# Convolutions of the latent tokens begun ahead of the layer's other convolutions, and a skip row by products

## The chip, the cores and the metric

The kernel is one program on 1 core of a Trainium2 chip. The metric is the device time of one execution in microseconds (us). The core's engines run side by side, each with its own in-order queue: TensorE (PE, matrix products; its weight loads are shown apart as PEld), VectorE (DVE), ScalarE (ACT), GpSimd (POOL) and SyncE (SP), which issues most DMAs.

## The reference

A backbone of two layers over 2,048 latent tokens and 256 context tokens, 1,024 wide. Layer 0 is attention beside a Hyena branch (two gated long convolutions), layer 1 two kinds of local attention. What the change touches lies in layer 0:

```python
def hyena_branch(u, conv_w, conv_b, w1, b1, w2, b2, freq, w3, d_skip):
    n = u.shape[1]
    filt = hyena_filters(n, w1, b1, w2, b2, freq, w3)
    uc = centred_depthwise_conv(u, conv_w, conv_b)
    parts = jnp.split(uc, HYENA_ORDER + 1, axis=-1)
    z = parts[0]
    for o in range(HYENA_ORDER):
        z = parts[o + 1] * bidir_long_conv(z, filt[:, o, 0], filt[:, o, 1], d_skip[o])
    return z

def bidir_long_conv(z, h_fwd, h_bwd, d_skip):
    n = z.shape[1]
    taps = jnp.concatenate([h_fwd, jnp.zeros_like(h_fwd[:1]), h_bwd[:0:-1]], axis=0)
    taps = taps * lax.rsqrt(jnp.sum(taps * taps, axis=0, keepdims=True) + EPS)
    zf = jnp.fft.rfft(z.astype(jnp.float32), n=2 * n, axis=1)
    tf = jnp.fft.rfft(taps, n=2 * n, axis=0)
    y = jnp.fft.irfft(zf * tf[None], n=2 * n, axis=1)[:, :n]
    return (y + z.astype(jnp.float32) * d_skip.astype(jnp.float32)).astype(z.dtype)
```

The modulation of each layer is `silu(cond) @ w_ada + b_ada`, split into shift, scale and gate; the projection is `modulated_norm(x) @ w_in`.

## The kernel before

Layer 0's projection runs in three groups of tokens (GRP: 768 each, as blocks of 512 and 256). For a group, `ln0` normalizes and transposes the tokens into `hT`; `kvq` makes keys, values and queries (products `psA`); `us` makes the 1,536 columns of the Hyena branch, 512 at a time, into `u0` in DRAM; `gates` makes two gates of 512 columns into `g0` (both products `psB`, L222; DVE or ACT empty the banks, L339 to L342). A product of two fp32 numbers is three products of fp32r halves, so each piece of `w_in` is loaded (`wraw`), rounded on ACT (`whi`, L243) and its rest made on POOL (`wlo`, L244). Three raw pieces of 256 KB are in flight.

`filters` (L450 on), during group 0 and 1, makes the long filters. Their first tap gets the skip weight: `d_skip` divided by the filter's norm. The norm is one number per channel; its channels lie across partitions, four to a partition (`ssv`, 128x4), while the tap's row (`first`) has 512 channels on one partition. L524 writes the four columns to DRAM (`rD`), L526 reads them back as a row, L528 loads the skip weights, L529 and L530 multiply and add. That is done four times: two filters, for the context (`ctxt` 1) and for the latent tokens (0).

Between groups 1 and 2 the program has the context's attention and Hyena branch and then, in pool `ad1`, the modulation's sums: `ada_sum` (L94, L95) multiplies the conditioning with `w_ada`'s last 1,024 columns of layer 0 and all 3,072 of layer 1. The three PSUM tiles `pa` that hold the sums are the whole of tag "x" (3 banks) in pool `xp`. The weights come through two slots of 128 x 3,072 (`adaw`), 1.5 MB each.

`gate_convs` convolves the last 512 columns of `u0` (pieces of 512 tokens, `gu` and `gy`) into `zG`. `latent_conv` convolves the other two parts: a unit is one block of 128 channels and a half of the tokens, loaded with a margin (`u`, 512.5 KB). ACT scales the middle tap (L721), DVE adds the two others (L723), all three writing the view `prm`, in which token n*64+s stands at s*32+n, so that neighbouring tokens are 128 bytes apart. There are 16 units: two parts, two halves of the channels (`ch`), two blocks in each and two halves of the tokens. PE transposes the result (`ptz`, L733); part 0 is stacked (`zst`, L380, L381), put through the first transform (`hpA`, L669, L670, in tag "x") and stored in `XA`; part 1 is stored in `zD`. The attention of layer 0 and the rest of the Hyena branch follow behind the first maxima (`pm`, L888), at about 1,180 us.

The kernel is written for a build that sets the order of instructions on each engine itself: a scheduler goes by the place in the program as priority, by what each instruction needs, and by its own durations. So work from several places of the program stands interleaved on an engine. Slots of a tile are given out in turn (`bufs`): a load into one waits, on the queue that issues it, until the last use of what was there.

## Time and profile before

| | us |
|---|---|
| median of three timed runs | 3899.59 |
| lowest, highest | 3898.86, 3904.81 |
| the profiled execution | 3905.59 |
| its span, first to last instruction | 3903.8 |
| PE busy | 3627.0 (93%) |
| DVE busy | 2305.7 (59%) |
| ACT busy | 1802.8 (46%) |
| POOL busy | 1733.5 (44%) |

Busy time is the union of an engine's instructions; issuing a DMA or waiting does not count. A releaser is what ended an engine's idle time. PEclk is the clock granted to PE, as a share of 2.4 GHz; a stretch at 0.5 runs at 1.2 GHz.

### The profile page before, as it was taken

Reading aid. Unit: us, or ns where it says so; the run is one execution under the profiler, and the core shown is the slowest. Engines: PE = TensorE matmul, PEld = TensorE weight load, DVE = VectorE, ACT = ScalarE, POOL = GpSimd, SP = SyncE. Lnnn points to the kernel's source line nnn. Section 1 sums busy time; section 2 is a strip of 40 time slices with the busy share of each in tenths; the row PEclk is TensorE's granted clock in tenths of the full one; section 3 lists DMA queues with packets and bytes.
Section 4 is the critical chain, followed back from the end, with each engine's and each line's share of the span. In section 5 each row is a group of like instructions: output and inputs, shape, how many; then the busy total and the mean of one; then the engine's idle time right before and its main releaser. Section 6 shows DMA issues by size and latency. Waiting matters only on the chain.

```text
span 3903.8 us, 57140 instructions
## 1 busy us (share of the span) xinstructions
PE 3627.0 (93%) x20080; PEld 2615.3 (67%) x20080; DVE 2305.7 (59%) x4370; ACT 1802.8 (46%) x3482; POOL 1733.5 (44%) x1433
## 2 busy tenths in 40 slices
PE   6799989997788999999998989999998999999999
PEld 2588767756574554455545657887876878888887
DVE  6754762626877775677664338286158267677622
ACT  4554652413535665566453334344233266666610
POOL 1444552213245786767797555353244222132310
PEclk9899999999898999999999999999999999999999
DMA  6444344465567555343343454555465375365355
GB/s 197 93 135 132 134 119 119 135 215 191 164 182 221 172 163 185 119 144 117 108 161 112 135 159 139 168 168 152 139 191 160 118 180 139 91 161 133 112 175 168
DMA packets 536337, 586.23 MB, mean 150 GB/s; under 512 B 71318, under 2 KB 362448, under 8 KB 531954
## 3 DMA queue, kind: packets, MB, share of 16 engines
q1 hardware_dynamic: 519778, 551.12, 48.5%
q10 hardware_dynamic: 13856, 25.18, 1.7%
q0 software_dynamic: 2416, 6.29, 0.6%
q8 instruction: 158, 2.59, 0.3%
q14 instruction: 129, 1.06, 0.1%
HBM read 389.63 MB, written 192.76 MB: 149 GB/s over the span
## 4 chain that ended last, share of the span: by engine, by line
PE 59%; DVE 8%; DMA 5%; issue 5%; ACT 3%; POOL 2%; SPq 0%; ACTq 0%; POOLq 0%; DVEq 0%
PE psB L222 8%; PE pso L222 7%; PE psA L222 6%; PE po L994 6%; PE npt L1569 4%; PE no L1581 4%; PE pS L975 4%; PE pm L888 3%; PE pS L976 3%; PE ns L1550 2%; PE ns L1556 2%; PE hpX L802 1%; PE hpC L795 1%; PE hpH L807 1%; DMA wraw<-in_w_in_dram 1%
## 5 line engine op out<-in xcount | busy, mean ns | idle before, releaser
L244 POOL TENSOR_TENSOR wlo<-wraw,whi 128x512 fp32r<-128x512 f32 x368 | 500.9, 1376 | 832.8 <-ACT whi L243 657.5
L989 POOL TENSOR_TENSOR pacc<-pacc,Pt 128x512 f32<-128x512 f32 x512 | 646.0, 1284 | 193.1 <-ACT Pt L977 191.4
L222 PE MATMUL psB<-hT,whi 128*128 128x512 f32 (+1 forms) x2560 | 667.1, 350 | 29.5 <-DVE u L714 8.9
L222 PE MATMUL psA<-whi,hT 128*128 128x512 f32 (+1 forms) x1952 | 571.3, 373 | 34.1 <-DVE u L717 11.3
L222 PEld LDWEIGHTS psB<-hT,whi 128*128 128x128 f32 x2560 | 451.9, 193 | 107.6 <-issue 13.1
L889 DVE TENSOR_REDUCE mx<-pm 128x1 f32<-128x512 f32 (+1 forms) x640 | 389.6, 631 | 185.5 <-PE pm L888 181.3
L977 ACT ACTIVATE Pt<-pS 128x512 f32<-128x512 f32 x576 | 332.9, 597 | 351.8 <-PE pS L976 326.1
L222 PE MATMUL psB<-hT,wlo 128*128 128x512 f32 (+1 forms) x1280 | 442.2, 351 | 8.0 <-POOL wlo L244 7.8
L222 PEld LDWEIGHTS psA<-whi,hT 128*128 128x128 f32 x1952 | 356.8, 193 | 103.5 <-DVE u L717 11.5
L243 ACT CAST whi<-wraw 128x512 fp32r<-128x512 f32 x368 | 222.0, 618 | 312.3 <-DMA wraw<-in_w_in_dram 141.4
L222 PE MATMUL psA<-wlo,hT 128*128 128x512 f32 (+1 forms) x976 | 356.6, 370 | 0.8 <-POOL wlo L244 0.5
L222 PE MATMUL pso<-whi,oy 128*128 128x512 f32 x1088 | 344.2, 395 | 9.1 <-DMA oy<-yT 8.2
L975 PE MATMUL pS<-Q,K 128*128 128x512 f32 x576 | 331.2, 575 | 10.2 <-ACT Pt L977 9.5
L994 PE MATMUL po<-Pt,V 128*64 128x512 f32 x1152 | 287.2, 621 | 0.0
L222 PEld LDWEIGHTS psB<-hT,wlo 128*128 128x128 f32 x1280 | 245.9, 193 | 46.8 <-POOL wlo L244 12.1
L1569 PE MATMUL npt<-ident,np 128*128 128x128 f32 x1488 | 258.2, 283 | 3.3 <-DVE ggt L1153 1.9
L975 PEld LDWEIGHTS pS<-Q,K 128*128 128x128 f32 x576 | 110.1, 191 | 205.2 <-issue 99.8
L222 PEld LDWEIGHTS pso<-whi,oy 128*128 128x128 f32 x1088 | 205.9, 190 | 60.4 <-issue 7.6
L976 PE MATMUL pS<-Q,K 65*128 65x512 f32 x576 | 231.9, 403 | 5.8 <-DMA Q<-mr 5.8
L888 PE MATMUL pm<-K,Q 128*128 128x512 f32 x600 | 217.3, 384 | 17.3 <-DVE mx L889 16.0
L222 PE MATMUL pso<-wlo,oy 128*128 128x512 f32 x544 | 213.7, 395 | 1.2 <-POOL wlo L244 1.2
L222 PEld LDWEIGHTS psA<-wlo,hT 128*128 128x128 f32 x976 | 188.8, 194 | 31.4 <-POOL wlo L244 2.4
(342 smaller groups left out, 6500.4 us busy)
## 6 DMA issues: line engine op xcount, KB each, us to landing
wraw<-in_w_in_dram SPq DMA_DIRECT2D x312, 256.0 KB
oy<-yT SPq DMA_DIRECT2D x72, 512.0 KB
qk<-tq SPq DMA_DIRECT2D x50, 512.0 KB
fA<-fev SPq DMA_DIRECT2D x64, 256.0 KB
hxb<-XA SPq DMA_DIRECT2D x64, 256.0 KB
hfb<-fA SPq DMA_DIRECT2D x64, 256.0 KB
XC<-hevc ACTq DMA_DIRECT2D x64, 256.0 KB
hdi<-XC SPq DMA_DIRECT2D x64, 256.0 KB
```

Of the source, the lines that this page charges most:

```text
L222: T.matmul(ps, a(x, kt), b(y, kt), start=(kt == 0 and n == 0), stop=(kt == 7 and n == 2))
L243: S.copy(hi, w)
L244: G.tensor_tensor(out=lo, in0=w, in1=hi.bitcast(F32), op=ALU.subtract)
L888: T.matmul(pm[:, :n], self.q1[:, h, qt * P:(qt + 1) * P], self.K1(c0, n), start=True, stop=True)
L889: V.tensor_reduce(out=self.mx[:, u, c:c + 1], in_=pm[:, :n], axis=AX.X, op=ALU.max)
L975: T.matmul(s, K1[kv][:, kt * P:(kt + 1) * P], q1[:, h, :], start=True, stop=False)
L976: T.matmul(s, K2[kv][:, kt * P:(kt + 1) * P], q2[:, h, :], start=False, stop=True)
L977: S.activation(pt[:, h, :], s, AF.Exp)
L989: G.tensor_tensor(out=acc[1][:, h], in0=acc[1][:, h], in1=p[:, h], op=ALU.add)
L994: T.matmul(po[64 * h:64 * h + 64, :], vt[:, kt, kv * 64:kv * 64 + 64], p[:, h, :], start=(kt == 0), stop=(kt == 17))
L1569: T.transpose(pt[:, i, :], self.p[h][:, (i0 + i) * P:(i0 + i + 1) * P], ident)
L1581: T.matmul(B["po"][64 * h:64 * h + 64, self.k, :], vt[:, kt, 64 * h:64 * h + 64], self.pT[h, i // 4][:, i % 4, :], start=(i == 0), stop=(i ...
```

## The change

1. The skip row: the four norms stay on their partitions, are multiplied there with the skip weights (`skip`, loaded once at the start as 128x4 for each filter), and four products with the identity (`pskip`) lay them along one row of a PSUM bank, from which DVE adds them to the first tap. `rD` and its loads go.
2. The latent convolutions: ACT's pass and DVE's first write a plain tile `uy` in token order; DVE's second writes the permuted `uc` from it. `uc` has 2 slots in place of 4, `u` 2 in place of 3.
3. Their place: `latent_conv` is called once for each part, part 0 behind the first two blocks of columns of group 2, part 1 behind the third, in a pool (`lc`) that is open beside the modulation's weights. All 16 gate convolutions follow behind the first gate of group 2; before, eight stood ahead of group 2 and eight behind `kvq`.
4. The modulation's weights come as 32 tiles of 128 x 1,024 in two slots, in place of 11 loads into two of 128 x 3,072.

```diff
--- before.py
+++ after.py
@@ -154,7 +154,6 @@
-    rD = dr.tile([4, 512], F32, tag="rD", name="rD")
@@ -443,12 +442,14 @@
         add("dsc", t, (t, C['dsc']))
         D["dA"] = t = scr(sb, "dA")[:, 0:P]
         ld.append(lambda t=t: nc.sync.dma_start(t, C['dftAf']))
+        t = new("skip", P, 2, 4)
+        add("skip", t, *[(t[:, o], I['hy_skip'][0, o].rearrange("(k p) -> p k", p=P)) for o in range(2)])
...
@@ -521,13 +522,11 @@
                 V.tensor_scalar(out=v, in0=pt[:, 0:4], scalar1=EPS, scalar2=None, op0=ALU.add)
                 rsqrt(sb, rc[ctxt][:, o, :], v, 4, "sst")
                 V.tensor_tensor(out=v, in0=v, in1=rc[ctxt][:, o, :], op=ALU.mult)
-                nc.sync.dma_start(rD[2 * ctxt + o].rearrange("(k p) -> p k", p=P), v)
-                v = scr(sb, "ssq")[0:1]
-                nc.sync.dma_start(v, rD[2 * ctxt + o:2 * ctxt + o + 1])
-                ds_ = scr(sb, "dskip")[0:1]
-                nc.sync.dma_start(ds_, I['hy_skip'][0, o:o + 1, :])
-                V.tensor_tensor(out=v, in0=v, in1=ds_, op=ALU.mult)
-                V.tensor_tensor(out=first[o][0:1, :], in0=first[o][0:1, :], in1=v, op=ALU.add)
+                V.tensor_tensor(out=v, in0=v, in1=skip[:, o], op=ALU.mult)
+                pt = ps.tile([P, 512], F32, tag="x", name="pskip", bufs=3)
+                for k in range(4):
+                    T.matmul(pt[0:1, k * P:(k + 1) * P], v[:, k:k + 1], ident, start=True, stop=True)
+                V.tensor_tensor(out=first[o][0:1, :], in0=first[o][0:1, :], in1=pt[0:1, :], op=ALU.add)
                 behind(o, 0, first[o])()
@@ -698,18 +697,22 @@
-    def latent_conv(sb, ps, pool2, ztile, etile):
-
-
+    def latent_conv(sb, ps, pool2, ztile, etile, parts, D={}):
+
+
+        if convw[0] is None:
+            convw[0] = conv_weights(0)
         w = convw[0]
-        dA = first_stage(sb)[0]
-        for part, ch in [(p, h) for p in range(2) for h in range(2)]:
+        if "dA" not in D:
+            D["dA"] = first_stage(sb)[0]
+        dA = D["dA"]
+        for part, ch in [(p, h) for p in parts for h in range(2)]:
             ucs = []
             for ct in (2 * ch, 2 * ch + 1):
                 k = part * 4 + ct
-                uc = sb.tile([P, 64, 32], F32, tag="uc", name="uc", bufs=4)
+                uc = sb.tile([P, 64, 32], F32, tag="uc", name="uc", bufs=2)
                 for hf in range(2):
-                    u = sb.tile([P, 1026], F32, tag="u", name="u", bufs=3)
+                    u = sb.tile([P, 1026], F32, tag="u", name="u", bufs=2)
                     if hf == 0:
                         V.memset(u[:, 0:1], 0.0)
                         nc.sync.dma_start(u[:, 1:], u0[k, :, 0:1025])
@@ -717,10 +720,11 @@
                         V.memset(u[:, 1025:1026], 0.0)
                         nc.sync.dma_start(u[:, 0:1025], u0[k, :, 1023:2048])
                     prm = uc.rearrange("p s n -> p n s")[:, 16 * hf:16 * hf + 16, :]
-                    v = [u[:, j:j + 1024].rearrange("p (n s) -> p n s", s=64) for j in range(3)]
-                    S.activation(prm, v[1], AF.Identity, bias=w[:, k, 3:4], scale=w[:, k, 1:2])
-                    for j in (0, 2):
-                        V.scalar_tensor_tensor(out=prm, in0=v[j], scalar=w[:, k, j:j + 1], in1=prm, op0=ALU.mult, op1=ALU.add)
+                    y = sb.tile([P, 1024], F32, tag="y", name="uy", bufs=2)
+                    S.activation(y, u[:, 1:1025], AF.Identity, bias=w[:, k, 3:4], scale=w[:, k, 1:2])
+                    V.scalar_tensor_tensor(out=y, in0=u[:, 0:1024], scalar=w[:, k, 0:1], in1=y, op0=ALU.mult, op1=ALU.add)
+                    V.scalar_tensor_tensor(out=prm, in0=u[:, 2:1026].rearrange("p (n s) -> p n s", s=64), scalar=w[:, k, 2:3],
+                                           in1=y.rearrange("p (n s) -> p n s", s=64), op0=ALU.mult, op1=ALU.add)
                 ucs.append(uc.rearrange("p s n -> p (s n)"))
             cs = slice(256 * ch, 256 * ch + 256)
             for g in range(0, 16, 2):
@@ -1228,8 +1232,8 @@
-        def us():
-            for b in range(3):
+        def us(bs=(0, 1, 2)):
+            for b in bs:
                 pj.cols(768 + 512 * b, False, u0[4 * b:4 * b + 4], True)
 
@@ -1286,40 +1290,47 @@
             ctx_hyena(fs, xp)
-        with ExitStack() as s2:
-            fs = s2.enter_context(tc.tile_pool(name="ad1", bufs=1))
-            bt = fs.tile([P, 512], F32, tag="s", name="adab", bufs=3)[0:6]
-            nc.sync.dma_start(bt, I['b_ada'][0].rearrange("(j c) -> j c", j=6))
-            pa = [xp.tile([P, 512], F32, tag="x", name=f"ada{i}", bufs=3) for i in range(3)]
-            wg = []
-            for k in range(0, 8, 3):
-                n = min(3, 8 - k)
-                w = fs.tile([P, 3072], F32, tag="adaw", name="adaw", bufs=2)
-                nc.sync.dma_start(w[:, :1024 * n].rearrange("p (k c) -> p k c", c=1024), I['w_ada'][0, k * P:(k + n) * P, 2048:].rearrange("(k p) c -> p k c", p=P))
-                wg += [[w[:, c:c + 512] for c in (1024 * i, 1024 * i + 512)] for i in range(n)]
-            ada_sum(pa[2:], bt, 4, lambda kt: wg[kt])
-            ada_gates(0, pa[2])
-            head = ada_head(1, fs, "s", 3)
-            ada_sum(pa[:2], head[1], 0, lambda kt: ada_rows(1, kt, [fs.tile([P, 3072], F32, tag="adaw", name="adaw", bufs=2)]))
-            ada_gates(1, pa[1])
-            ada_mods(1, fs, "s", 3, xp, ("x", 3), head[0], pa[0])
+        s2 = ExitStack()
+        fs = s2.enter_context(tc.tile_pool(name="ad1", bufs=1))
+        bt = fs.tile([P, 512], F32, tag="s", name="adab", bufs=3)[0:6]
+        nc.sync.dma_start(bt, I['b_ada'][0].rearrange("(j c) -> j c", j=6))
+        pa = [xp.tile([P, 512], F32, tag="x", name=f"ada{i}", bufs=3) for i in range(3)]
+
+        def ada_w():
+            return fs.tile([P, 1024], F32, tag="adaw", name="adaw", bufs=2)
+
+        def wg(kt):
+            w = ada_w()
+            nc.sync.dma_start(w, I['w_ada'][0, kt * P:(kt + 1) * P, 2048:])
+            return [w[:, :512], w[:, 512:]]
+
+        ada_sum(pa[2:], bt, 4, wg)
+        ada_gates(0, pa[2])
+        head = ada_head(1, fs, "s", 3)
+        ada_sum(pa[:2], head[1], 0, lambda kt: ada_rows(1, kt, [ada_w() for _ in range(3)]))
+        ada_gates(1, pa[1])
+        ada_mods(1, fs, "s", 3, xp, ("x", 3), head[0], pa[0])
         ln0(1, xs1)
         kvq()
         us()
         xs2 = ln_in(GRP[2][0])
         gates()
+        ln0(2, xs2)
+        us((0, 1))
+        ls = s2.enter_context(tc.tile_pool(name="lc", bufs=1))
+
+        def conv(part):
+            latent_conv(ls, xp, ps, lambda i: (sb, ls)[i].tile([P, 512], F32R, tag="lnh", name="zst", bufs=2),
+                        lambda: sb.tile([P, 1024], F32, tag="lnx", name="zev", bufs=6), (part,))
+
+        conv(0)
+        us((2,))
+        conv(1)
+        s2.close()
+        gates((0,))
         with ExitStack() as s2:
-            gate_convs(s2.enter_context(tc.tile_pool(name="gc", bufs=1)), (0, 1))
-        ln0(2, xs2)
-        us()
-        with ExitStack() as s2:
-            fs = s2.enter_context(tc.tile_pool(name="lc", bufs=1))
-            latent_conv(fs, xp, ps, lambda i: (sb, fs)[i].tile([P, 512], F32R, tag="lnh", name="zst", bufs=2),
-                        lambda: sb.tile([P, 1024], F32, tag="lnx", name="zev", bufs=6))
-        gates((0,))
+            gate_convs(s2.enter_context(tc.tile_pool(name="gc", bufs=1)), range(4))
         kvq()
-        with ExitStack() as s2:
-            gate_convs(s2.enter_context(tc.tile_pool(name="gc", bufs=1)), (2, 3))
```

The order on DVE at the end of the last filter of the latent tokens, from the norm (`ssv`) to the split of the first tap (`st`); `bo<-psB` empties a bank of the projection. Before:

```order
L523 TENSOR_TENSOR ssv<-ssv,rc_102 128x4
L585 TENSOR_TENSOR cwx_7367<-cw,rc_102 128x16
L587 TENSOR_SCALAR cwx_7367<-cwx_7367 128x16
L342 COPY bo<-psB 128x512 x2
L529 TENSOR_TENSOR ssq<-ssq,dskip 1x512
L530 TENSOR_TENSOR tap<-tap,ssq 1x512
L457 TENSOR_TENSOR st<-tap,st 128x512
```

After:

```order
L524 TENSOR_TENSOR ssv<-ssv,rc_101 128x4
L584 TENSOR_TENSOR cwx_8106<-cw,rc_101 128x16
L525 TENSOR_TENSOR ssv<-ssv,skip 128x4
L586 TENSOR_SCALAR cwx_8106<-cwx_8106 128x16
L529 TENSOR_TENSOR tap<-tap,pskip 1x512
L458 TENSOR_TENSOR st<-tap,st 128x512
```

One operation of 128x4 stands where two bank copies and a product on one partition stood, and the addition takes its row from PSUM.

The order on SP at the start of the modulation's sums; `u<-bo` stores columns of the projection, `wraw` loads its weights, `u<-u` loads a convolution's unit. Before:

```order
L1298 DMA adaw<-in_w_ada_dram 128x3x1024 x2
L83 DMA adab<-in_b_ada_dram 6x512
L343 DMA u_88<-bo 128x512 x2
L1298 DMA adaw<-in_w_ada_dram 128x2x1024
L343 DMA u_88<-bo 128x256 x2
L77 DMA adaw<-in_w_ada_dram 128x3072
L242 DMA wraw<-in_w_in_dram 128x512
```

After:

```order
L1304 DMA adaw<-in_w_ada_dram 128x1024 x2
L83 DMA adab<-in_b_ada_dram 6x512
L342 DMA u_87<-bo 128x512
L661 DMA dA<-in_dftA_const 128x128
L718 DMA u<-u_87 128x1025
L342 DMA u_87<-bo 128x256 x2
L1304 DMA adaw<-in_w_ada_dram 128x1024
L721 DMA u<-u_87 128x1025
L1304 DMA adaw<-in_w_ada_dram 128x1024
L718 DMA u<-u_87 128x1025
L241 DMA wraw<-in_w_in_dram 128x512
```

Units of the convolution are loaded between the modulation's pieces; before, the first of them came some 45 rows later.

The order on DVE at the first units of the latent convolution (`dAl` is the rest of the first transform's matrix). Before, behind eight gate convolutions:

```order
L342 COPY bo<-psB 128x256
L714 MEMSET u 128x1
L666 TENSOR_TENSOR dAl<-dA,dAh 128x128
L342 COPY bo<-psB 128x256 x2
L723 SCALAR_TENSOR_TENSOR uc<-u,cwx_7367,uc 128x16x64 x5
L717 MEMSET u 128x1
```

After, ahead of the end of the modulation's sums:

```order
L341 COPY bo<-psB 128x512 x2
L717 MEMSET u 128x1
L720 MEMSET u 128x1
L341 COPY bo<-psB 128x256 x2
L665 TENSOR_TENSOR dAl<-dA,dAh 128x128
L725 SCALAR_TENSOR_TENSOR uy<-u,cwx_8106,uy 128x1024
L726 SCALAR_TENSOR_TENSOR uc<-u,cwx_8106,uy 128x16x64
```

The passes come in pairs of a plain and a permuted one. Counted over both orders, four last passes, six first ones and four stacks stand ahead of the sums' end after the change and none before it, and 280 column products of 512 with 288 of 256 stand there, where 135 and 192 did.

## Rows read from the trace of the kernel before

**Rows 1.** Stretches: length, busy PE, PEld, DVE, ACT, POOL (instructions), clock, DMA, GB/s.

```profile
112.00:152.00 40.00, 24.20 (x118) 19.49 (x117) 20.87 (x65) 13.08 (x32) 10.11 (x12) 0.79 0.43 56
560.00:610.00 50.00, 42.42 (x199) 35.39 (x200) 12.91 (x31) 7.94 (x16) 10.26 (x9) 0.83 0.40 92
808.00:895.00 87.00, 87.00 (x462) 52.40 (x461) 10.60 (x30) 8.73 (x16) 15.17 (x13) 1.00 0.73 255
895.00:1180.00 285.00, 226.54 (x1121) 176.71 (x1119) 217.59 (x326) 125.55 (x200) 106.21 (x91) 0.88 0.59 179
```

**Rows 2.** DVE in order of time: start, us, operation [idle before it, releaser].

```profile
135.78 0.68 DVE L529 TENSOR_TENSOR ssq<-ssq,dskip 1x512 f32<-1x512 f32 x1 [8.26 <-DMA dskip<-in_hy_skip_dram]
...
597.27 0.68 DVE L529 TENSOR_TENSOR ssq<-ssq,dskip 1x512 f32<-1x512 f32 x1 [8.70 <-DMA dskip<-in_hy_skip_dram]
```

**Rows 3.** PE in order of time, around its gaps in the first two stretches.

```profile
126.02 0.62 PE L222 MATMUL psA<-whi,hT 128*128 128x512 f32 x2
...
141.19 0.45 PE L209 MATMUL pt<-ident,qn 128*128 128x128 f32 x1 [10.23 <-DVE tq L214]
141.29 1.20 PE L222 MATMUL psA<-whi,hT 128*128 128x512 f32 x2
...
147.83 0.80 PE L562 MATMUL pA<-st,dAh 128*128 128x512 f32 x1 [4.48 <-ACT st L456]
...
575.64 1.22 PE L222 MATMUL psB<-hT,whi 128*128 128x512 f32 x2 [4.03 <-ACT whi L243]
...
599.42 0.79 PE L562 MATMUL pA<-st,dAh 128*128 128x512 f32 x1 [3.42 <-ACT st L456]
```

**Rows 4.** SP's waits at line L526: count, ns min/median/max, first and last start.

```profile
L526 SPq EVENT_SEMAPHORE  x3: 17/17/8746, 124.1 to 563.7; - x3
```

**Rows 5.** PE's waits in 895 to 1180: us in total, times, longest.

```profile
PE hpA L669 <- DVE zst L381: 12.1, 1, 12.1
PE psA L222 <- DVE u L717: 11.3, 1, 11.3
PE psB L222 <- DVE u L714: 8.9, 1, 8.9
```

**Rows 6.** Single operations by line: count, ns min/median/max, first and last start, shapes.

```profile
L723 DVE SCALAR_TENSOR_TENSOR uc<-u,cwx,uc x32: 2109/2252/3335, 937.3 to 1076.6; 128x1024 f32<-128x1024 f32 x32
...
L698 DVE SCALAR_TENSOR_TENSOR gy<-gu,cwx,gy x32: 736/752/1857, 899.0 to 1147.9; 128x512 f32<-128x512 f32 x32
...
L596 DVE SCALAR_TENSOR_TENSOR ucc<-ucx,cwx,ucc x12: 473/484/1569, 692.2 to 722.9; 128x256 f32<-128x256 f32 x12
...
L381 DVE TENSOR_TENSOR zst<-ptz,zst x32: 673/688/695, 971.5 to 1069.9; 64x512 fp32r<-64x512 f32 x32
...
L721 ACT ACTIVATE uc<-u,cwx x16: 2090/2165/2330, 935.0 to 1067.1; 128x1024 f32<-128x1024 f32 x16
...
L696 ACT ACTIVATE gy<-gu,cwx x16: 798/816/823, 898.1 to 1141.8; 128x512 f32<-128x512 f32 x16
...
L519 PE MATMUL pss<-ones,acc x32: 168/250/353, 114.4 to 581.9; 128*128 128x1 f32 x32
```

**Rows 7.** Pieces of the chain that ended last: start, us, what, instructions.

```profile
845.26 5.44 PE psB L222 x23
850.69 1.84 PE ada L95 x12
...
878.20 4.51 PE psB L222 x36
...
931.10 3.85 DMA u<-u
...
1174.38 14.69 DMA Q<-q
```

**Rows 8.** DVE's waits in 895 to 1180: us in total, times, longest.

```profile
DVE gy L698 <- ACT gy L696: 22.4, 10, 5.8
...
DVE uc L723 <- ACT uc L721: 7.4, 3, 4.3
```

More of the change, by code (lines that the diff above doesn't have):

```diff
@@ L450, in filters @@
     def filters(sb, ps, D):
-        zf, w1, pc, w2, dl, dscc, w3, dsc, dA = (D[k] for k in ("zf", "w1", "pc", "w2", "dl", "dscc", "w3", "dsc", "dA"))
+        zf, w1, pc, w2, dl, dscc, w3, dsc, dA, skip = (D[k] for k in ("zf", "w1", "pc", "w2", "dl", "dscc", "w3", "dsc", "dA", "skip"))
         def new(nm, *shape, tag=None, bufs=1, dt=F32R):
```

## The prediction

> **What bounds the kernel now.** I read the busy time by stretches first, then TensorE's waits in the stretches with gaps, then what the releasing engine was doing. TensorE (PE) is busy for 93% of the span, so only stretches in which it stands idle, or runs at half clock after standing idle, have anything to give. Three do [rows 1]. In 112 to 152 us PE is busy 24.20 of 40 us at a granted clock of 0.79. In 560 to 610 us it is busy 42.42 of 50 at 0.83. In 895 to 1180 us, the end of the first projection stage, it is busy 226.54 of 285 at 0.88, while VectorE (DVE) works 217.59 of the 285. Between them, in 808 to 895 us, PE is full (87.00 of 87, clock 1.00) and DVE does 10.60 us of work. After 1180 us I expect the order to be the old one but for details, so its 2,724 us count as unchanged.
>
> The two early stretches are stalls on one step: the skip row of the filters. DVE stands 8.26 and 8.70 us before L529, waiting for loads that stand behind a round trip of four numbers per partition through DRAM [rows 2]. PE's gaps behind them are 10.23, 4.48, 4.03 and 3.42 us [rows 3]. The 4.03 is one step further off: SyncE (SP), which issues the DMAs in order, stood 8.75 us (8746 ns, the longest of three) before the load of the row just written [rows 4], and the weights that PE needed next were queued behind it. In the third stretch the long PE waits are 12.1 us for `zst`, 11.3 us for L717 and 8.9 us for L714 [rows 5]. The last two are a memset that only marks the place: on DVE's in-order queue it stands among the convolution's updates (L723), and what PE wanted, a PSUM bank to be emptied, stood behind those.
>
> **The change part by part.**
>
> *Skip row.* Removed are twelve DMAs, the four round trips, and eight DVE operations on one partition. Added are two small loads at the start, four multiplications of 128x4, four additions on one partition that read PSUM, and sixteen products on PE. The nearest row for a product is the 250 ns of L519 [rows 6], so 16 x 0.25 = 4.0 us at most; a product also moves 128 columns, so I do not go below half of that. The new wait: the products stand in PE's queue behind a chain on DVE, and projections are queued behind them. In the new order of the last filter 33 column products, some 7.8 us at 0.236 us each (5.44 us for 23) [rows 7], stand between the sum of squares and the skip products, about what the chain of small operations wants, so I cost the wait at nothing; without that cover it is the chain itself, a few microseconds four times. Gain, upper bound: the four gaps make 10.23 + 4.48 + 4.03 + 3.42 = 22.2 us. Half clock follows them, as two projection products show that take 1.20 us behind the gap against 0.62 before [rows 3]. The clock that was missing, times PE's busy share, is 0.21 x 24.20 + 0.17 x 42.42 = 12.3 us [rows 1]. So 34.5 - 4 = 30 us. Lower bound: only the second place pays (7.45 us, and a third of the clock), 10 us, because DVE and ACT have plenty to do after the first. I take **20 us**, between the bounds, since all four gaps go but each leaves a chain that still has to run.
>
> *Token order.* Each of the 16 units had one ACT pass and two DVE passes, all writing the permuted view. Now the ACT pass and the first DVE pass are contiguous, and only the last writes permuted. A DVE update of 256 columns takes 484 ns and of 512 columns 752 [rows 6], 268 more for 256, so 1,024 contiguous ones come to an estimated 752 + 2 x 268 = 1.29 us against 2.25 now. For the last pass the bounds are 1.29 (if the permuted read was the cost) and 2.25 (if the write is). The ACT pass settles which is nearer: it reads contiguously, writes permuted, and takes 2.17 us where twice the 816 ns of 512 columns would be 1.63 [rows 6]. So I take 2.25. DVE saves 16 x 0.96 = 15 us in all, ACT about 16 x 0.5 = 9.
>
> *Begun earlier.* The order after puts four of the 16 units (first pass on six), four stacks and some ten more evacuations of column banks before the end of the modulation's sums, when DVE was nearly free [rows 1]. The other side: 145 column products of 512 and 96 of 256 move with them, ahead of the sums' end, and 16 transposes. At 0.236 and 0.125 us (5.44 for 23, 4.51 for 36) [rows 7] that is 34 + 12 + 2 = 48 us, so the sums that ended at 895 end at about 943. PE is full in that stretch and should stay so. What is left behind it on DVE: 217.6 us now, less 4 units x 4.5 = 18.0, less the cheaper passes of the rest (ten first passes at 1.29 and twelve last ones at 2.25 make 39.9 where 24 old ones made 54.0) 14.1, less 14 stacks and evacuations at up to 0.69 each [rows 6], some 8: 177.5 us. DVE's idle time there is 285 - 217.6 = 67.4 us now. Of that 22.4 us were the gate convolutions and 7.4 us the latent ones, both waiting for ACT [rows 8]; in the new order gate convolutions stand singly between other work, which covers both. That leaves 37.6, and the stretch lasts 177.5 + 37.6 = 215 us, to 943 + 215 = 1158 instead of 1180: **22 us** gained. Bounds: with all of the old idle time it ends at 1188, 8 us later than now; with none left, at 1121, 59 us earlier. What is next behind DVE there is PE, whose own products in it I put at about 155 us.
>
> *Gate convolutions* are moved, not changed: the 16 stand behind the sums, spread over the rest. Their loads and stores pass through SP's queue among the filter products' stores; that is in the 37.6.
>
> Sum: 20 + 22 = 42 us. The profiled execution took 3905.59 us, 1.8 over its span and 6.0 over the median of the three timed runs. I take the difference to the median as it is: 3899.6 - 42 = **3858 us**.
>
> **The rivals.**
>
> *The modulation's weights in small pieces starve PE (slower).* Before, 11 loads of up to 1.5 MB went into two slots; now 32 of 512 KB go into two slots, and each waits on SP until PE has used the piece two before, with the projection's own weights queued behind it. PE's queue is in order, so a piece that is late stops all of PE. From the first sum to the last PE has 263 x 0.236 + 250 x 0.125 + 72 x 0.31 = 116 us of work (1.84 us for 12 rows, two to a product) [rows 7], 3.6 us for a piece, so a load has 7.2 us. For it: a load of the same size took 14.69 us at the end of the stage, when the DMA engines were full. Against it: another took 3.85 us [rows 7], and PE did not wait at all with the large pieces [rows 1]. If a load takes L, the stretch takes 16 L; it eats the whole 42 us from 16 L = 158, that is L = 9.9 us. At 11 us the kernel takes 3900 + 18 = 3918.
> The Trainium skill, page "SBUF — State Buffer", section "The DMA setup-cost knee", speaks against the change here: each transfer pays about 2 us whatever its size, so one should use the largest single transfers. By its fit, as an estimate, 32 pieces cost 32 x 3.2 = 102 us where the 11 cost 61. That is 41 us more of DMA time, but still below the work that covers it; no row here shows a load of this form, and the 3.85 us of the nearest is close to the page's 3.2.
>
> *DVE waits as before.* Earlier starts only move the waits: the part from the sums on keeps its 67.4 us of idle DVE and ends at 1188. Then the skip row alone pays, about 3900 - 20 + 8 = 3888, or 3880 without the extra 8. For it: the first transforms cannot start before the sums end, because the three PSUM banks that they use hold the sums, and the order shows all 64 of their products behind them. So the change does only a part of what it says: a quarter of the units is ahead of the sums.
>
> *The skip row moves its stall.* PE's gap at 130 to 141 us lies in a stretch in which DVE and ACT are well used too; if they were the bound, nothing is gained by the shorter chain, and 3900 - 22 = 3878 remains.
>
> *PE becomes the bound.* DVE's idle time goes entirely and the stage ends at 1121 to 1130: 3900 - 20 - 55 = 3825.
>
> **How the numbers follow.** The forecast (both parts pay, 3840 to 3870) has 0.48. DVE waits as before 0.18, skip row moves its stall 0.11, PE the bound 0.13, pieces starve PE 0.06, the rest (both small gains fail together) 0.04. The range reaches from just under the PE-bound case to the worse form of the second rival: 3820 to 3888. A measurement of this kernel can tell about 0.2%, 8 us, from no change. Faster by more than that: 0.48 + 0.13 + 0.11 + most of the 0.18 = 0.87; within: 0.07; slower: 0.06.
>
> **What would show it right or wrong.** In the profile after: no DVE wait for a DMA at the skip row and no PE gap over 3 us at 130 to 150 and 570 to 600 us; the first pass near 1.3 us and the last near 2.25 us on DVE; the sums' end near 943 less the 20 us gained before, with PE full and no wait for `adaw`; first attention scores some 42 us earlier than the 1180 of now. A last pass near 1.3 us would mean that the read was the cost; waits of PE for `adaw` would mean the first rival. It is wrong as a whole if the time from the stage's end on changes by more than a few microseconds, since I counted nothing there.

## The result and the profile after

The changed kernel takes 3858.07 us (median), the kernel before 3899.23 beside it: ratio 0.9892, 95% interval 0.9875 to 0.9909. That is 41.2 us for the forecast's 42. The profiled execution took 3855.73 us with a span of 3854.0. It is 49.9 us below the profiled one of before: that one lay 6 us over its median and this one 2 us under its own, so differences between the two traces run some 8 us high.

The stretches that answer to [rows 1], in the changed kernel's trace (columns as there; each stretch is set where the same work stands in this trace):

```profile
112.00:152.00 40.00, 39.52 (x216) 32.76 (x216) 35.87 (x98) 21.41 (x51) 23.16 (x24) 0.97 0.31 97
540.00:590.00 50.00, 48.55 (x302) 42.33 (x302) 14.13 (x37) 12.67 (x22) 16.95 (x13) 1.00 0.51 140
773.00:923.50 150.50, 150.50 (x735) 94.90 (x733) 38.09 (x53) 27.28 (x42) 34.56 (x24) 1.00 0.66 211
923.50:1127.70 204.20, 173.36 (x848) 132.07 (x848) 176.21 (x305) 92.41 (x175) 85.48 (x80) 0.89 0.68 208
```

The first two lines are the places of the skip row. PE was busy 24.20 of 40 us and 42.42 of 50 before, at clocks of 0.79 and 0.83; now it is nearly full, at 0.97 and 1.00. The third line is the modulation's sums. They took 90.8 us with PE full (803.1 to 893.9) and take 150.5 with PE full. The fourth is the rest of the stage, from the sums' end to the first attention score: 286.6 us before, 204.2 now. DVE works 176.21 us in it, against a forecast of 177.5. PE works 173.36, at a clock of 0.89, where the prediction had put about 155.

The skip row itself, first the four additions and what DVE waited for ahead of them, then PE in order of time around one group of products:

```profile
L529 DVE TENSOR_TENSOR tap<-tap,pskip x4: 665/676/676, 132.1 to 569.2; 1x512 f32<-1x512 f32 x4
its engine sat idle before it (us, times) until:
  PE pskip L528: 7.3, 2
```

```profile
129.00 0.39 PE L221 MATMUL psA<-wlo,hT 128*128 128x512 f32 x1
129.32 1.03 PE L528 MATMUL pskip<-ident,ssv 128*1 128x128 f32 x8
130.29 1.05 PE L520 MATMUL pss<-ones,acc 128*128 128x1 f32 x8
131.20 0.42 PE L208 MATMUL pt<-ident,qn 128*128 128x128 f32 x2
```

No DMA ends a wait there any more [rows 2]. DVE still waits for PE, 7.3 us in two places, and PE does not wait in return. Each product shows as two instructions, and the eight of one filter take about 1 us: 4 us for all four filters, the price in the prediction.

The three passes of a latent unit, ACT, first and last on DVE (columns as in [rows 6]):

```profile
L724 ACT ACTIVATE uy<-u,cwx x16: 1225/1242/1252, 788.0 to 1056.7; 128x1024 f32<-128x1024 f32 x16
...
L725 DVE SCALAR_TENSOR_TENSOR uy<-u,cwx,uy x16: 1269/1285/2324, 789.3 to 1061.3; 128x1024 f32<-128x1024 f32 x16
...
L726 DVE SCALAR_TENSOR_TENSOR uc<-u,cwx,uy x16: 1964/2138/3087, 790.6 to 1065.4; 128x1024 f32<-128x1024 f32 x16
```

PE's waits from 926 to 1154, answering to [rows 5]:

```profile
PE pS L980 <- DMA Q<-mr: 10.9, 1, 10.9
PE ptz L737 <- DVE uc L726: 10.8, 2, 6.3
PE hpA L668 <- DVE zst L380: 7.3, 4, 3.6
PE psA L221 <- ACT vt L361: 6.9, 3, 3.5
```

The two waits for a memset (11.3 and 8.9 us) have shrunk to 1.6 us. There is none for `adaw`. DVE's waits for ACT in the same window, 22.4 and 7.4 us before [rows 8]:

```profile
DVE uy L725 <- ACT uy L724: 3.0, 1, 3.0
DVE gy L697 <- ACT gy L695: 2.4, 3, 1.1
```

Of one kernel below, `e_row`, the trace is of an execution of 5931 us at a granted clock of 0.61, and its median is that of its three other executions, at 0.97 to 0.98.

### The profile page after: what moved, and what is told of

Same layout as the page of the kernel before. It is cut to its first block, busy times and chain, and to the rows that moved or that the text cites. A ratio compares the mean times of both kernels' runs of the same rounds, so it can differ in the third digit from the quotient of the medians.

```text
span 3854.0 us, 57179 instructions
## 1 busy us (share of the span) xinstructions
PE 3628.1 (94%) x20112; PEld 2607.1 (68%) x20112; DVE 2284.9 (59%) x4370; ACT 1784.9 (46%) x3480; POOL 1735.3 (45%) x1433
## 4 chain that ended last, share of the span: by engine, by line
PE 69%; DVE 13%; issue 5%; DMA 5%; ACT 4%; POOL 2%; SPq 1%; ACTq 0%; DVEq 0%; POOLq 0%
PE psB L221 16%; PE pso L221 7%; PE po L998 6%; PE psA L221 5%; PE npt L1580 4%; PE no L1592 4%; PE pS L979 4%; PE pm L892 3%; PE pS L980 3%; PE ns L1561 2%; PE ns L1567 2%; DMA wraw<-in_w_in_dram 2%; PE hpX L806 1%; PE hpC L799 1%; PE hpH L811 1%
## 5 line engine op out<-in xcount | busy, mean ns | idle before, releaser
L221 PE MATMUL psB<-hT,wlo 128*128 128x512 f32 (+1 forms) x1280 | 433.8, 344 | 0.0
L892 PE MATMUL pm<-K,Q 128*128 128x512 f32 x600 | 217.0, 384 | 16.6 <-DVE mx L893 16.5
```

Source lines behind the costliest of these rows:

```text
L221: T.matmul(ps, a(x, kt), b(y, kt), start=(kt == 0 and n == 0), stop=(kt == 7 and n == 2))
L892: T.matmul(pm[:, :n], self.q1[:, h, qt * P:(qt + 1) * P], self.K1(c0, n), start=True, stop=True)
```

## The experiments

The edits compared are S (skip row), T (token order), E (convolutions begun earlier, which brings the modulation's weights in small pieces because the convolutions' buffers take the room). In the table, "context" is the end of PE's last transposition `pty` of the context tokens' part, "sums" the end of the transposition `adat` of the modulation's sums, and "score" the first product `pS` of the attention; these are read from each trace. The stretch is from sums to score, and DVE's idle time is that stretch less DVE's busy time in it. The intervals are those of the ratio to before; before itself took 3899.07 to 3899.91 us in all the comparisons. An interval is 5 to 8 us wide on either side, so by estimate a difference of less than some 8 us between two rows is not clear of the spread. E also holds the move of the gate convolutions and the smaller number of buffers; no run takes these apart.

| kernel | median us | ratio, 95% interval | context | sums | score | stretch | DVE idle |
|---|---|---|---|---|---|---|---|
| before | 3899.9 | | 803.1 | 893.9 | 1180.5 | 286.6 | 68 |
| `e_skip` (S) | 3878.8 | 0.9939, 0.9926 to 0.9951 | 773.6 | 864.0 | 1152.9 | 288.9 | 72 |
| `e_order` (T) | 3885.6 | 0.9959, 0.9946 to 0.9972 | 801.5 | 892.3 | 1162.4 | 270.1 | 62 |
| `e_skord` (S, T) | 3851.4 | 0.9880, 0.9865 to 0.9895 | 771.8 | 862.1 | 1128.6 | 266.5 | 65 |
| `e_pieces` (pieces alone) | 3951.1 | 1.0134, 1.0113 to 1.0155 | 800.0 | 947.8 | 1224.4 | 276.6 | 65 |
| `e_place` (S, E) | 3878.4 | 0.9943, 0.9929 to 0.9956 | 773.0 | 928.3 | 1154.3 | 226.0 | 41 |
| `e_conv` (T, E) | 3879.3 | 0.9948, 0.9935 to 0.9960 | 799.7 | 947.8 | 1153.4 | 205.6 | 27 |
| after (S, T, E) | 3858.1 | 0.9892, 0.9875 to 0.9909 | 773.0 | 923.5 | 1127.7 | 204.2 | 28 |
| `e_half` (after, pieces halved) | 3871.1 | 0.9926, 0.9912 to 0.9941 | 774.1 | 940.1 | 1150.2 | 210.1 | 31 |
| `e_noskip` (after, no skip) | 3852.2 | 0.9877, 0.9864 to 0.9891 | 750.3 | 902.0 | 1120.6 | 218.6 | 34 |
| `e_row` (after, skip as a row) | 3857.9 | 0.9887, 0.9871 to 0.9903 | | | | | |
| `e_zev` (after, ACT evacuates) | 3848.7 | 0.9869, 0.9856 to 0.9883 | 772.3 | 922.8 | 1121.1 | 198.3 | 29 |
| `e_pool` (`e_zev`, memsets on POOL) | 3853.8 | 0.9886, 0.9871 to 0.9901 | 773.4 | 923.9 | 1121.7 | 197.8 | 28 |
| `e_big` (`e_zev`, larger pieces) | 3832.1 | 0.9827, 0.9813 to 0.9842 | 774.3 | 895.5 | 1105.8 | 210.3 | 39 |

**The skip row alone (`e_skip`).** The four pieces of the change that touch the skip row, put into the kernel before:

```diff
-                nc.sync.dma_start(rD[2 * ctxt + o].rearrange("(k p) -> p k", p=P), v)
...
-                V.tensor_tensor(out=v, in0=v, in1=ds_, op=ALU.mult)
...
+                V.tensor_tensor(out=v, in0=v, in1=skip[:, o], op=ALU.mult)
...
+                    T.matmul(pt[0:1, k * P:(k + 1) * P], v[:, k:k + 1], ident, start=True, stop=True)
```

> The kernel before with the skip row's edit alone: the four round trips through DRAM go, the skip loads move to the start, sixteen identity products come in. Theory (the skip row pays by itself, 20 us in the prediction, about 25 by the trace of the changed kernel): 3870 to 3880 us, the last sum of squares of the filters some 22 us earlier than before's 582, PE gaps over 3 us at 112 to 152 and 560 to 610 gone, everything behind it shifted by the same amount. Rival (the stall only moves, the early gain of the changed kernel comes from its other order): 3892 to 3900 us, with new PE waits in those stretches. Rival (the skip row carries the whole change): 3858 to 3862 us.

It is 21.1 us faster, with the last sum of squares ending at 561.1 for 582.3. Around the second place (540 to 590 us) PE is busy 49.02 of 50 us at a clock of 1.00. In its trace PE's waits from 121 to 171 us are all that is left of gaps of 10.23 and 4.48 us [rows 3] (us in total, times, longest):

```profile
PE pA L561 <- DVE st L458: 0.5, 1, 0.5
PE psA L221 <- ACT vt L361: 0.5, 1, 0.5
PE pt L208 <- POOL qn L201: 0.2, 1, 0.2
```

The theory holds, and the rival that the stall moves falls. In the traces the context part ends 26 to 30 us earlier wherever the skip row is changed. Of the 29.5 us in this pair, 26.6 are left at the end of the two profiled executions; the rest of the way to 21.1 is that before's lay 6 us over its median.

**The convolutions' part alone (`e_conv`).** The changed kernel with the old skip row (the diff above, reversed).

> The changed kernel with the old skip row put back (round trips through DRAM, skip loads behind them), so the convolutions' part of the change alone. Theory (the stage part pays 22 us by itself): 3874 to 3882 us, with before's PE gaps at 112 to 152 and 560 to 610 back, and the stretch from the first sum of the modulation to the first attention score some 22 us shorter than before's 367. Rival (the skip row carries all): 3895 to 3900. Rival (the two parts need each other, because the stage gain depends on when the first projection's loads begin): under 10 us gained, with the sums' end to the stage's end as long as before.

It is 20.6 us faster than before, as the theory said, and 21.3 slower than the changed kernel. The two halves of the change add up.

**Token order alone (`e_order`).** In the kernel before, at the old place:

```diff
-                uc = sb.tile([P, 64, 32], F32, tag="uc", name="uc", bufs=4)
+                uc = sb.tile([P, 64, 32], F32, tag="uc", name="uc", bufs=3)
...
-                    S.activation(prm, v[1], AF.Identity, bias=w[:, k, 3:4], scale=w[:, k, 1:2])
...
+                    y = sb.tile([P, 1024], F32, tag="y", name="uy", bufs=2)
+                    S.activation(y, u[:, 1:1025], AF.Identity, bias=w[:, k, 3:4], scale=w[:, k, 1:2])
...
```

> The kernel before with token order alone: one ACT pass and the first DVE pass contiguous, only the last pass permuted, at the old place. One buffer fewer for the permuted tile (three for four), so that the new one fits. Theory (DVE sets the end of the first projection stage, so its 15 us fewer count in large part): 3886 to 3892 us. Rival (the waits close over it; the gain of the stage is the earlier start): 3896 to 3900 us. Rival (token order is the whole stage gain): 3876 to 3880 us.

It is 14.3 us faster, close to the 15 us of DVE time that the passes save. The stretch in its trace:

```profile
892.30:1162.40 270.10, 231.27 (x1125) 179.72 (x1125) 207.64 (x337) 112.34 (x200) 104.64 (x93) 0.89 0.61 190
```

DVE works 207.64 us in it, 11 less than before, and the stretch is 16.5 shorter.

**The place without token order (`e_place`).** The changed kernel with the three permuted passes of before (the last lines of the diff above, reversed).

> The changed kernel with all three passes permuted again, as before (ACT 2.17 us for 1.24, first DVE pass 2.25 for 1.29), everything else as changed. Theory (twelve units stand in the DVE-bound part, 12 x 0.96 = 11.5 us of DVE): 3864 to 3872 us, 6 to 14 slower than the changed kernel's 3858. Rival (place alone does it, DVE has idle time to take the longer passes): 3855 to 3861 us. Rival (token order is the stage gain): 3876 to 3882 us.

It is 20.3 us slower than the changed kernel, and no faster than the skip row alone (3878.4 and 3878.8). That is the rival "token order is the stage gain", in the middle of its range; the theory's 6 to 14 us was too small.

**Skip row and token order, place as before (`e_skord`).** The edits of `e_skip` and `e_order` together.

> The kernel before with the skip row's edit and token order, all convolutions at their old place (three buffers for the permuted tile, as in the run of token order alone). Against the changed kernel this leaves out the earlier start with its small pieces. Theory (additive: 3878.8 for the skip row alone, less the 14.3 of token order alone): 3861 to 3868 us, so that the earlier start is worth 3 to 10 us on top of token order. Rival (the earlier start is worth nothing, as it was with the permuted passes): 3856 to 3860. Rival (token order pays only with the earlier start): 3872 or more.

Measured 3851.4, below every theory: the changed kernel without its earlier start is 6.7 us faster than with it by the medians, and the same in the profiled executions (3855.8 and 3855.7). The intervals of the two ratios overlap (0.9865 to 0.9895, 0.9875 to 0.9909), so it is not shown that the earlier start costs time; but a gain of the 8 us that the forecast's sum leaves for it is not there. The two traces reach the first score within 1 us of each other (1128.6 and 1127.7).

**The pieces alone (`e_pieces`).** The kernel before with the weights in pieces as the changed kernel has them, nothing moved:

```diff
-                w = fs.tile([P, 3072], F32, tag="adaw", name="adaw", bufs=2)
...
+                return fs.tile([P, 1024], F32, tag="adaw", name="adaw", bufs=2)
...
-            ada_sum(pa[:2], head[1], 0, lambda kt: ada_rows(1, kt, [fs.tile([P, 3072], F32, tag="adaw", name="adaw", bufs=2)]))
+            ada_sum(pa[:2], head[1], 0, lambda kt: ada_rows(1, kt, [ada_w() for _ in range(3)]))
```

> The kernel before with one part of the change alone: the modulation's weights of the sums at 804 to 894 in 32 pieces of 512 KB into two slots of 1,024 columns, for 11 loads into two slots of 3,072. Nothing else moves. Theory (each change of TensorE between modulation and projection products costs 0.58 us by the changed kernel's trace, and TensorE is full there): 12 pairs become 32, 20 x 0.58 = 11.7 us, so 3908 to 3914 us for before's 3899, with the sums' end some 10 to 12 us later and TensorE still full. Rival (the earlier sums' end is not what the stage waits for, DVE is): sums' end later, but 3897 to 3903. Rival (small loads starve TensorE): its waits for adaw, over 3915.

It is 51 us slower, four times the theory's price, and not because PE starves. The sums and the stretch behind them:

```profile
800.00:947.80 147.80, 147.80 (x717) 92.91 (x716) 16.45 (x36) 18.34 (x32) 30.36 (x24) 1.00 0.61 192
947.80:1224.40 276.60, 203.64 (x890) 151.31 (x888) 211.76 (x329) 117.85 (x187) 83.42 (x80) 0.77 0.55 165
```

PE is full to the sums' end and never waits for `adaw`. The sums end 54 us later because the order has 717 instructions ahead of their end where before had 482: between each two pieces stand projection products. They are work brought forward, but it buys little behind the sums, because the stretch there is paced by DVE (211.76 us of work, 218.76 in before): with 237 fewer column products in it, PE is busy for 203.64 us where before had 227.72, but stands idle for longer and at a clock of 0.77 for 0.88. And in no run did the latents' first transform start before the sums' last product. The small part is a real price. The modulation products' rows, first of before (803 to 894), then of `e_big`, of `e_pieces` and of `e_half` (each in its sums):

```profile
L95 PE MATMUL ada<-adaw,sil 128*32 128x512 f32 x128 | 27.1, 600 | 0.0
```

```profile
L95 PE MATMUL ada<-adaw,sil 128*32 128x512 f32 x128 | 29.5, 605 | 0.0
```

```profile
L95 PE MATMUL ada<-adaw,sil 128*32 128x512 f32 x128 | 37.8, 605 | 0.0
```

```profile
L95 PE MATMUL ada<-adaw,sil 128*32 128x512 f32 x128 | 63.8, 605 | 0.0
```

The same 128 instructions keep PE busy for 27.1, 29.5, 37.8 and 63.8 us when their weights come in 11, 24, 32 and 64 pieces (12, 25, 33 and 60 groups between projections in the traces; the changed kernel's row is that of `e_pieces`). So 10.7 us of the 54 are the groups themselves. The price is not the same for each group: 13 more groups cost 2.4 us from before to `e_big`, and 27 more cost 26 from `e_pieces` to `e_half`. Why the order puts more projections between smaller pieces, no run shows; the loads' issues wait on SP until PE has used the piece two before (44.1 us in 17 waits, where before had 28.9 in 8).

**Pieces halved (`e_half`).**

```diff
-            return fs.tile([P, 1024], F32, tag="adaw", name="adaw", bufs=2)
+            return fs.tile([P, 512], F32, tag="adaw", name="adaw", bufs=4)
...
-        ada_sum(pa[:2], head[1], 0, lambda kt: ada_rows(1, kt, [ada_w() for _ in range(3)]))
+        ada_sum(pa[:2], head[1], 0, lambda kt: ada_rows(1, kt, [ada_w() for _ in range(6)]))
```

> The changed kernel with the modulation's weights in pieces half as large: 64 loads of 256 KB into four slots of 512 columns, for 32 of 512 KB into two of 1,024 (same memory). In the changed kernel's trace a modulation product that follows a projection product ends 0.547 us after it, against 0.154 to 0.170 behind another modulation product, and a projection product of 512 behind a modulation product 0.429 against 0.229: 0.58 us for each pair of changes, at 32 changes where before had 12. Theory (each piece costs such a pair): up to 32 more pairs, 19 us, sums' end near 940 for 923.5, time 3870 to 3877 us. Rival (the changes cost nothing by themselves, the order's other work fills them): 3856 to 3861, sums' end within 3 us. Rival (small pieces starve TensorE): waits of TensorE for adaw, and over 3880.

It is 13 us slower than the changed kernel, with the sums' end at 940.1, as the theory said, and no waits for `adaw`. That the sums' end agrees is luck in part: the groups' price grows by more than the theory's 19 us (26 by the rows above), and 60 fewer projection products stand ahead of the sums' end, some 14 us.

**No skip row (`e_noskip`).** The changed kernel without lines 525 to 529.

> The changed kernel without the skip row's small chain: the multiplication by the skip, the sixteen products and the four additions are left out (the loads stay). Its output lacks the skip term. In the changed kernel the products show as 32 instructions of 0.272 us, 8.7 us of TensorE, twice the 4 of the prediction. Theory (TensorE is full around them, so they lie on the path): 3848 to 3852 us, 6 to 10 faster than the changed kernel's 3858. Rival (they stand in time that was idle anyway): 3856 to 3860. Rival (the chain ahead of them still stalls TensorE): below 3846.

It is 5.9 us faster, at the edge of the theory's range and within the spread, and not as the theory said: the 8.7 us there add up instructions that overlap (8 take 1.03 us, so 4 us in all). The context part ends 23 us earlier, but with 179 fewer column products ahead of it (2,397 for 2,576), so this is another order and not the chain's price. 14 of the 23 us are lost behind the sums, where the order now has the first transposition of the latents at 875 us instead of 801. What the chain alone costs cannot be read from this run.

**The skip as a row (`e_row`).**

```diff
+                ds_ = scr(sb, "dskip")[0:1]
+                nc.sync.dma_start(ds_, I['hy_skip'][0, o:o + 1, :])
...
-                V.tensor_tensor(out=v, in0=v, in1=skip[:, o], op=ALU.mult)
...
+                V.tensor_tensor(out=v, in0=pt[0:1, :], in1=ds_, op=ALU.mult)
```

> The changed kernel with the skip loaded as a row, 2 KB in one piece, just ahead of the sum of squares, and multiplied in as a row behind the products (one DVE operation of 1x512, 0.67 us by the addition beside it, for one of 128x4 at 0.16), so the loads of single numbers at the start are gone. The start of the changed kernel is late: first transposition of the norms at 59.9 us for 56.2, first sum of squares at 120.6 for 114.4. Theory (the two loads of single numbers at the start cost that): start as before's, 3851 to 3856 us. Rival (the order of the first products on TensorE costs it, whatever the loads): start as in the changed kernel, 3857 to 3861.

The median is the changed kernel's, but the three executions reach from 3852.2 to 3859.2 us, over both ranges, so the time does not decide. In the trace the first transposition of the norms comes at 59.6 us, for 59.9 with the loads of single numbers and 56.2 before. That does not clear the loads. PE's products ahead of it, first in before, then in the changed kernel:

```profile
53.37 0.65 PE L480 MATMUL p<-h,w 64*64 64x512 f32 x2 [0.59 <-ACT h L399]
```

```profile
54.43 1.12 PE L481 MATMUL p<-h,w 64*64 64x512 f32 x2 [3.29 <-ACT h L398]
```

The wait for ACT is 2.5 to 4.0 us in all kernels that have these loads, 0.59 to 0.89 in those with the old row, and 0.95 in `e_row`. So with the loads the wait goes, as the theory would have it. What `e_row`'s trace keeps is the other half, the duration: 1.11 us for these two instructions, near the 1.12 of the changed kernel, where the clock granted from 54 to 62 us was 0.50 for before's 1.00. (For `e_row` the records give 1.00 there, which its durations do not bear out.) A long duration there needs no new skip row: `e_order`, whose edit touches nothing at the start, has 1.1 us too, at a clock of 0.60, and its first sum of squares at 118.1 us for 114.4. How much of the late start the loads cost stays open.

**Evacuations on ACT (`e_zev`).**

```diff
-                    (S.copy if h else V.tensor_copy)(ev[:, h], pA)
+                    S.copy(ev[:, h], pA)
```

> The changed kernel with all 32 evacuations of the latents' first transform on ACT (half are on DVE): DVE loses 16 x 0.69 = 11 us in the last part of the stage, ACT gains 16 x 0.59 = 9. DVE is busy for 174 of the 202 us from 926 to 1128, ACT for 92. Theory (DVE's work sets the end of the stage): 3847 to 3853 us, with the first attention score 5 to 11 us earlier than the changed kernel's 1127.7. Rival (DVE's waits and the order set it, or TensorE does): 3855 to 3862.

It is 9.4 us faster than the changed kernel (6.7 in the profiled executions), as the theory said for a stretch that DVE sets:

```profile
922.80:1121.00 198.20, 173.43 (x848) 131.86 (x847) 169.38 (x289) 101.13 (x191) 85.22 (x80) 0.87 0.70 214
```

DVE's work falls from 176.21 to 169.38 us, the stretch from 204.2 to 198.2, while PE's work stays (173.36 and 173.43).

**Memsets on POOL (`e_pool`).**

```diff
-                        V.memset(u[:, 0:1], 0.0)
+                        G.memset(u[:, 0:1], 0.0)
...
-                        V.memset(u[:, 1025:1026], 0.0)
+                        G.memset(u[:, 1025:1026], 0.0)
```

> The changed kernel with the latents' evacuations all on ACT (3848.7 us by itself) and the latents' two boundary memsets on POOL instead of DVE, as the gate convolutions have them. Theory (on DVE's in-order queue a memset waits for its buffer, and what stands behind it waits too): 3843 to 3848 us. Rival (those waits are gone already, TensorE waited for it for 1.6 us in all): 3847 to 3851. Rival (POOL is late with them, its queue is long): over 3852.

The score comes at 1121.7 us for `e_zev`'s 1121.1, so nothing changes in the stage. The median is 5.2 us above `e_zev`'s, which the two intervals do not separate; in the traces 2.5 of it lie behind the score. A loss is not shown.

**Larger pieces (`e_big`).** Pieces of up to 1,536 columns for 1,024, with one buffer for the contiguous tile:

```diff
-            return fs.tile([P, 1024], F32, tag="adaw", name="adaw", bufs=2)
+            return fs.tile([P, 1536], F32, tag="adaw", name="adaw", bufs=2)
...
-        ada_sum(pa[:2], head[1], 0, lambda kt: ada_rows(1, kt, [ada_w() for _ in range(3)]))
+        ada_sum(pa[:2], head[1], 0, lambda kt: ada_rows(1, kt, [ada_w() for _ in range(2)]))
...
-                    y = sb.tile([P, 1024], F32, tag="y", name="uy", bufs=2)
+                    y = sb.tile([P, 1024], F32, tag="y", name="uy", bufs=1)
```

> The changed kernel with the latents' evacuations all on ACT (3848.7 us by itself) and the modulation's weights in pieces of up to 1,536 columns, 24 for 32; for the room the contiguous tile of the latents' convolution has one buffer for two. Theory (8 pairs of changes on TensorE fewer, 8 x 0.58 = 4.6 us, and one buffer is enough): 3842 to 3846 us, sums' end 4 to 5 us earlier. Rival (the one buffer makes ACT wait for DVE's last pass): 3849 or more, with the sums' end earlier all the same.

Measured 3832.1 us, 16.6 below `e_zev` and 26 below the changed kernel, the fastest of all. The gain is more than three times what the theory gave. Again the sums' end moves by far more than the groups' price:

```profile
774.30:895.50 121.20, 121.20 (x634) 77.33 (x632) 33.93 (x48) 20.91 (x32) 25.58 (x16) 1.00 0.72 239
895.50:1105.80 210.30, 193.12 (x949) 146.80 (x949) 171.05 (x294) 107.73 (x202) 95.49 (x88) 0.91 0.73 222
```

24 pieces for 32 end the sums 27 us earlier, with 634 instructions ahead of that end for 736, and lengthen what follows by 12. ACT does wait for DVE's last pass now (17.0 us in 9 waits), but ACT has the time. Whether larger pieces, or ACT's evacuations, pay as much without the earlier start, no run shows.

## Why the prediction was right

*Skip row: right in mechanism and size.* Forecast 20 between 10 and 30. Measured 21.1 alone and 21.3 on top of the rest; on top of token order alone it was 34.2 (`e_order` to `e_skord`), over the upper bound. The traces hold more than 20 (context 26 to 30 us earlier). The products took the 4 us that were put down for them, and PE did not wait for the chain. The prediction did not see the later start: the first sum of squares stands at 119 to 122 us in the kernels with the new loads and at 114 to 118 in those with the old row.

*Token order: mechanism right, share too small.* The durations were right: first pass 1.285 us for an estimate of 1.29, last pass 2.138 for 2.25, so the permuted write was the cost, as ACT had suggested. ACT's pass is 1.24 us, well under the estimated 1.63, so ACT saved 15 us for 9. The sum counted only 14.1 us of DVE's saving in the last stretch. Measured: 14.3 alone, 27.4 on top of the skip row, 20.3 on top of skip row and earlier start. Where it exceeds DVE's 15 us, the runs do not say why, and part may be spread; a unit also passes faster through its ACT pass, which no term counted.

*Begun earlier: the step that failed.* Of the forecast's 22 us for the stage, the 8 beyond token order's 14 were this edit's. By the runs it brings 6.3 us without the skip row, 0.4 with it but without token order, and costs 6.7 with both: nothing, within the spread. The two large terms were sized well and nearly cancel, as forecast. The sums took 60 us longer (forecast 48); the missing 12 are nearly the 10.7 of the modulation products in smaller groups, which the sum put at nothing. The stretch behind them fell to 204.2 (forecast 215), with 28 us of DVE idle time (forecast 37.6): the waits for ACT went from 22.4 and 7.4 us to 2.4 and 3.0, as argued. But the cause of the first term was wrong: the products ahead of the sums' end do not move with the convolutions. They move because the pieces are small. `e_pieces` has the same 147.8 us as `e_conv` without a single convolution moved, and 276 column products of 512 with 288 of 256 in them, where the changed kernel has 279 and 288. So the edit buys a stretch 62 to 65 us shorter (by the three pairs of the table that differ in it alone) and pays 57 to 65 us ahead of the sums' end for the room that it needs. `e_big` shows it from the other side.

*The total: right in part by luck.* In the order skip row, token order, earlier start the runs give 21.1 + 27.4 - 6.7 = 41.8 us where the forecast had 20 + 14 + 8: what token order gave more made up for what the earlier start did not give.

*The rivals.* "Small pieces starve PE" had the right suspect and the wrong mechanism. PE does not wait for a load; it is kept full of other work while the sums wait. The rival's sum of 116 us from the first sum to the last is 140 in the trace, because the modulation products, put at 22 us by a row of twelve in one group, take 45 in groups of mostly four. At the old place that costs 51 us, and the convolutions begun earlier cover it. The Trainium skill, page "SBUF — State Buffer", section "The DMA setup-cost knee", advises the largest single transfers where DMA is the bound. In direction the runs agree (11, 24, 32 and 64 pieces put the sums at 91, 121, 150 and 166 us), but PE was full in all of them, so the 2 us per transfer that it states is not what they show. "DVE waits as before" has its time, but not its mechanism, in `e_place`, the earlier start without token order: 3878.4 us for the rival's 3880, but with DVE idle for 41 us behind the sums and not 67. "PE becomes the bound" did not come about, but was near: PE was busy for 173.36 us of the last stretch, 3 us less than DVE. That DVE still set it is shown by `e_zev`, where 7 us less of DVE's work alone made it 6 us shorter.

*What was to be seen.* No PE gap over 3 us at the skip row, no wait for `adaw`, and a sums' end at 923.5 for "943 less 20". That last agreement is partly luck: the context part ended 30 us earlier for 20, and the sums took 12 us longer than forecast. The first score came 52.8 us earlier in the profiled pair, 45 after allowing for the 8 us by which that pair is apart from the medians. From there to the end both traces need nearly the same time, 2723.3 and 2726.3 us, as counted.

## What to carry to other kernels

A change that needs room takes it from somewhere: cost what gives the room by itself, at the old place, before crediting the move, since here the two nearly cancelled. When one engine's in-order queue paces a stretch, shortening its operations and handing some to an idle engine paid almost one for one, while starting the work earlier did not. A full engine does not show that its work is in the right order: look at when the result that the next stretch waits for is ready.

## What was not expected of the hardware

By the mean time from end to end in the traces of the sums (before and after), an instruction of a modulation product that follows a projection product ended 0.547 us after it, against 0.154 to 0.170 us behind another such instruction, and a projection product of 512 columns behind a modulation product 0.429 us after it, against 0.229 behind its own kind. So each group costs some 0.58 us more, which is 12 us for 20 groups, in line with the 10.7 of the rows above. It holds for these two kernels only: behind another such instruction it was 0.122 us in `e_big` and 0.390 in `e_half`, whose groups are mostly of two instructions. In order of time from the changed kernel, one such group of four between projections of 256 columns:

```profile
842.53 0.28 PE L221 MATMUL psB<-hT,whi 128*128 128x256 f32 x1
842.74 1.05 PE L95 MATMUL ada<-adaw,sil 128*32 128x512 f32 x4
843.72 0.38 PE L221 MATMUL psB<-hT,whi 128*128 128x256 f32 x1
```

An operation of 1,024 fp32 columns in rows of 128 partitions took 2.14 us on DVE with a permuted write (and reads in order) and 1.29 without, and 2.17 and 1.24 on ACT: the write's pattern alone cost 0.85 to 0.93 us on either engine.
